# Two heads at a time in the indexer and the sparse logits, the keys' low half on 64 rows of the array each

## The chip, the cores and the metric

The kernel runs on one NeuronCore of a Trainium2 chip. The metric is the device time of one execution in microseconds (us). Before the change the median of three runs is 2247.49 us (2243.25 to 2249.33). The kernel and its change are compared on the same inputs, and only the time is in question.

## What is computed

The reference is one layer of a decoder trunk on 1024 positions of width 1024: a SwiGLU block, a projection into two attention mixers, the gated merge of both, and a second SwiGLU block. Two places matter here, both in the first mixer (sparse attention). For each block of 128 queries:

```python
dots = jnp.einsum('bthd,bsd->bths', qi, k_idx)               # 8 heads of 64, one key for all heads
score = jnp.einsum('bths,bth->bts', jax.nn.relu(dots), wi)   # the indexer's score of each key
...                                                          # causal mask, the 256 best keys stay
logits = jnp.einsum('bthd,btkd->bthk', qa, kg) * (HEAD_DIM ** -0.5)
p = jax.nn.softmax(logits, axis=-1)
```

The kernel does not gather the chosen keys. It makes the logits of all keys up to the block's own and adds a bias that hides those not chosen. In both places eight heads of 64 numbers are multiplied with the same keys.

## The kernel before

All matmuls read their float32 operands in the fast one-pass form, which keeps fewer digits, so an operand is stored as a high part and a low part, the rest, and a product of two such operands is three matmuls: high by high, low by high, high by low (`mm3`, L308 to L310). Heads have only 64 rows, half of the array's 128. So for each head the query tile holds its high part in 64 rows and its low part in the other 64; the keys' high part is stored twice, once in each half of the rows, and so is the low part. One matmul with the keys' high tile then gives two of the three products at once, and one with the keys' low tile gives the third, along with the product of the two low parts, which is too small to matter. In `qstack` (L1512, L1514) head h has its high part in the rows of half h % 2, and its low part in the other half.

The order of the work is made while the program is built. Generators ("streams") such as `indexer`, `logits` or `outputs` yield before each step and name the engine and what they need; the class `Weave` keeps an estimated clock of every engine (`cost`, L112) and always takes the step that can start first, by rank where two can. Each engine then runs its instructions in that order. Everything between the two SwiGLU blocks is ordered so, in these stretches (times from the trace):

- **Index**, about 788 to 903 us. `indexer` (L1546) goes through blocks of queries 5, 4, 2, 7, 6, 3, in each through 8 heads, and in each head through pieces of at most 512 keys. A piece is two matmuls into one bank of PSUM, `psdot` (L1560 with the keys' high part `kih`, L1561 with the low part `kil`). `dot_out` takes the bank: ACT writes its positive part (`relu`, L1530), DVE multiplies it by the head's weight and adds it to the score (L1535, L1537). Between these, `fillers` puts projection work on PE that nothing waits for at once (`psf`, `psvb`: L308 to L310).
- **Search and stick-breaking**, about 903 to 1262 us. `topk` finds the 256th score by 31 steps, each one ACT pass per block (L1183) and two small DVE steps. `sticks` and `values` do the second mixer. `fillers` goes on with the gates (`psf` with weights `wg`).
- **Sparse attention**, about 1262 to 1474 us. `logits` (L1809) makes the logits of blocks 1, 0, 5, 4, 7, 6, 3, 2, head by head, again two matmuls for each piece of 512 keys into a bank `psL` (L1828, L1829). `logit_out` (L1792, DVE) adds the bias and writes `e`; `soft` exponentiates on ACT and scales on DVE (L1807). `latent_values` turns `e` by transposes on PE (`pspT`, L1883) and multiplies with the values (`pso`). `outputs` gives PE work in between: the projection of the second mixer (`psob`), then of the first (`psoa`), which waits for the first's results.

The banks `psdot`, `psz` and `psL` come from one ring, `ubank`, of three PSUM banks. The tiles `e` come from three rings, two of four and two tiles and later a third of two.

Of the kernel before, what the change touches and what calls it, by code (L numbers as in the profile page):

```python
# [10 lines left out]
F32 = mybir.dt.float32  # L11
# [10 lines left out]
PE, DVE, ACT, POOL, SP = "PE", "DVE", "Activation", "Pool", "SP"  # L22

P = 128
# [6 lines left out]
H = 8  # L31
HD = 64
# [61 lines left out]
class Weave:  # L94
# [17 lines left out]
    def cost(self, i, eng, outs, ins):  # L112

        n = max([a.free_size() for a in outs[:1] + ins], default=1)
        if eng == PE:
            return 0.01 + max(outs[0].free_size(), 240) / 2350, 0.0
        if eng == ACT:
            return 0.055 + n / 1190 + 0.31 * (len(outs) > 1), 0.1 + 0.1 * (len(outs) > 1)
        if eng == POOL:
            return 0.2 + n / 465 + (0.15 + 0.145 * n) * (n <= H), 0.0  # L120
        wide = [a for a in outs[:1] + ins if a.free_size() > H]
        if not wide:
            return 0.12 + 0.1 * (len(ins) > 1), 0.08
        if getattr(i, "is_tensor_tensor_scan", False):
            return 0.1 + n / 480, 0.08
        if len(outs) > 1:
            return 0.13 + n / 960, 0.05
        if len(wide) == 2 and not any(a.space == PSUM for a in wide):
            return 0.17 + n * (0.5 if any(a.dtype in (F32, F32R, I32) for a in wide) else 0.25) / 960, 0.08
        slow = getattr(i, "is_scalar_tensor_tensor", False) or len(ins) == 1 and len(outs[0].shape) == 2 and n > outs[0].free_size()  # L130
        return 0.07 + 0.06 * slow + 0.11 * (outs[0].shape[0] < P) + n / 960, 0.08
# [51 lines left out]
    def mark(self, name, *needs):  # L183
        self.marks[name] = needs
# [23 lines left out]
    def spawn(self, gen, rank=1, own=None):  # L208
        s = Stream(gen, rank, own or self.own)
        self.streams.append(s)  # L210
        self.step(s)
        return s
# [33 lines left out]
def trunk(ctx, tc, x, positions, g_ffn1, w1_gate, w1_up, w1_down, g_mix, w_in, g_cq, w_uq_a, w_q_idx,  # L246
          g_q_a, g_k_a, w_uv_a, w_o_a, w_o_b, w_out, g_ffn2, w2_gate, w2_up, w2_down, inv_freq, out):
    nc = tc.nc
# [18 lines left out]
    def sm(name, n=1, dt=F32, bufs=4):  # L267
        return small.tile([P, n], dt, name=name, bufs=bufs)
# [479 lines left out]
    def ring(pool):  # L748

        op = in_turn((wt, 4), (lambda name: pool.tile([P, 1024], F32R, tag="r", name=name, bufs=NR), NR))  # L750
        raw = in_turn((rawt, 2), (lambda name: pool.tile([P, 1024], F32, tag="raw", name=name, bufs=2), 2))
        return op, raw
# [6 lines left out]
    with tc.tile_pool(name="ring1", bufs=1) as rpool, tc.tile_pool(name="s1", bufs=1) as spool, tc.tile_pool(name="ps1", bufs=1, space=PSUM) as psum:  # L759
        op, raw = ring(rpool)  # L760
        bank = banks(psum)
        sums, pair = of(spool, "s", 5, 512), of(spool, "pair", 2, 512, F32R)
# [197 lines left out]
    with fp as fpool, fps as fpsum, psm as psum, tc.manual_schedule(  # L960
            engines={nc.tensor.engine, nc.vector.engine, nc.scalar.engine, nc.gpsimd.engine}):
        weave = Weave(nc)
        give, spawn, mark = weave.give, weave.spawn, weave.mark
# [29 lines left out]
        ubank, vbank, wbank = (ring_of(tiles_of(psum), tag, bufs, (P, 512)) for tag, bufs in (("u", 3), ("v", 2), ("w", 1)))  # L993
# [7 lines left out]
        score, here, HQ, KV, QA, BIAS = {}, {}, [], [], [], []  # L1001
# [319 lines left out]
        KX, QI, WQ = {}, {}, {}  # L1321
# [196 lines left out]
        def index_queries():  # L1518
# [4 lines left out]
            give(*WQ["qi"].parts)  # L1523
            mark("wqi")

        def dot_out(ps, i, h, c0, w, acc, before):
            yield ACT, ps, relus
            rt = relus("relu")
            r = rt[:, 0:w]
            nc.scalar.activation(r, ps[:, 0:w], AF.Relu)  # L1530
            give(ps)
            yield DVE, rt, before
            wv, ac = WI[:, i, h:h + 1], acc[:, c0:c0 + w]
            if h == 0:
                nc.vector.tensor_scalar(ac, r, wv, None, op0=ALU.mult)  # L1535
            else:
                nc.vector.scalar_tensor_tensor(ac, r, wv, ac, op0=ALU.mult, op1=ALU.add)  # L1537
            give(rt)
# [7 lines left out]
        def indexer():  # L1546

            for i in order:
                yield PE, "kidx", f"qi{i}"
                nk = (i + 1) * P  # L1550
                acc = keep(f"u{i}", f"u{i}", 1, shape=(P, nk))
                outs = {}
                for h in range(H):
                    for c0 in range(0, nk, 512):
                        w = min(512, nk - c0)
                        yield PE, ubank
                        ps = ubank("psdot")
                        lh = QI[i][:, h * P:(h + 1) * P]
                        x = max(w, 256)
                        nc.tensor.matmul(ps[:, 0:x], lh, KX["h"][:, c0:c0 + x], start=True, stop=False)  # L1560
                        nc.tensor.matmul(ps[:, 0:x], lh, KX["l"][:, c0:c0 + x], start=False, stop=True)  # L1561
                        outs[c0] = spawn(dot_out(ps, i, h, c0, w, acc, outs.get(c0)))
                give(QI[i])
                score[i] = acc
                mark(f"score{i}", spawn(score_out(i, acc, list(outs.values()))))
# [41 lines left out]
        pring, lefts = ring_of(rows_, "pt", 3, dt=F32R), ring_of(rows_, "left", 2)  # L1607
        arings = ring_of(s, "a0", 4, (P, 512)), ring_of(rows_, "a1", 4)
# [180 lines left out]
        def logit_out(lp, e, bias, c0, n_, m):  # L1789
            yield DVE, lp  # L1790
            c = slice(c0, c0 + n_)
            nc.vector.tensor_tensor_reduce(e[:, c], lp[:, 0:n_], bias[:, c], 1.0, LOW, op0=ALU.add, op1=ALU.max,  # L1792
                                           accum_out=m)
            give(lp, bias)
# [14 lines left out]
        def logits():  # L1809
            n = 0  # L1810
            yield PE, "sparse", "ka2"
            kah, kal = KV[:2]
            for b, i in enumerate(blocks):
                nk = (i + 1) * P
                yield PE, f"qa{b}", f"bias{b}"
                QS, bias = QA[b], BIAS[b]
                for h in range(H):
                    rings = [arings[1], lefts] + ([here["e"]] if "e" in here else [])
                    yield PE, rings
                    ring = min(rings, key=lambda r: weave.when((r,), PE))  # L1820
                    e, mx, outs = ring("e"), sm("mx", 2, F32, 8), []
                    for g, c0 in enumerate(range(0, nk, 512)):
                        yield PE, ubank
                        lp = ubank("psL")
                        n_ = min(512, nk - c0)
                        w = max(n_, 256)
                        lh = QS[:, h * P:(h + 1) * P]
                        nc.tensor.matmul(lp[:, 0:w], lh, kah[:, c0:c0 + w], start=True, stop=False)  # L1828
                        nc.tensor.matmul(lp[:, 0:w], lh, kal[:, c0:c0 + w], start=False, stop=True)  # L1829
                        outs.append(spawn(logit_out(lp, e, bias, c0, n_, mx[:, g:g + 1])))  # L1830
                    E[n] = e
                    mark(f"p{n}", spawn(soft(n, e, nk, mx, outs)), e)
                    n += 1
                give(QS)

        def o_out(op, b, g):
# [333 lines left out]
```

## Time and profile before

| | |
|---|---|
| median of three runs | 2247.49 us |
| the profiled execution's own time | 2252.81 us |
| its span, first to last instruction | 2251.0 us |
| granted TensorE clock, mean | 0.987 |
| PE busy | 2175.0 us, 10460 matmuls |
| DVE busy | 1541.6 us |
| ACT busy | 1116.5 us |

The profile is of one execution. A matmul's duration in it reaches beyond the start of the next, since matmuls are pipelined: what a matmul costs in a stream is the distance from its start to the next one's start. PE stands for matmuls, PEld for the loads of their left-hand operand, which run beside them. In a row of the tiles' view the three numbers after the colon are the least, median and largest duration in ns. In a row of the windows' view the first number after the window is its length, then come the busy time and the number of instructions of PE, PEld, DVE, ACT and POOL, the granted clock, the share of the DMA engines' time, and GB/s. In a row of the timeline stand the start, the duration, the engine, the line, the operation with its result and operands, and how many of them were merged; idle time before it stands in brackets. In a row of the waits stand the total, the number of times, and the longest.

### The profile page before, as it was taken

Reading aid. Unit: us, or ns where it says so; the run is one execution under the profiler, and the core shown is the slowest. Engines: PE = TensorE matmul, PEld = TensorE weight load, DVE = VectorE, ACT = ScalarE, POOL = GpSimd, SP = SyncE. Lnnn points to the kernel's source line nnn. Section 1 sums busy time; section 2 is a strip of 40 time slices with the busy share of each in tenths; the row PEclk is TensorE's granted clock in tenths of the full one; section 3 lists DMA queues with packets and bytes.
Section 4 is the critical chain, followed back from the end, with each engine's and each line's share of the span. In section 5 each row is a group of like instructions: output and inputs, shape, how many; then the busy total and the mean of one; then the engine's idle time right before and its main releaser. Section 6 shows DMA issues by size and latency. Waiting matters only on the chain.

```text
span 2251.0 us, 30640 instructions
## 1 busy us (share of the span) xinstructions
PE 2175.0 (97%) x10460; PEld 1810.2 (80%) x10460; DVE 1541.6 (68%) x2548; ACT 1116.5 (50%) x2169; POOL 840.3 (37%) x698
## 2 busy tenths in 40 slices
PE   7999899999999999899999899999999999999999
PEld 6778777888878988788888788878878888888877
DVE  5866675677876498687787688853476565658685
ACT  5433333334445258999988466533333333334443
POOL 3554454522336344211111323255255555442233
PEclk9999999999999999999999999999999999999999
DMA  5377677678676333665555523566223332359655
GB/s 170 99 225 210 206 220 207 188 248 281 204 209 175 110 121 136 207 170 162 163 148 166 207 92 99 176 222 224 66 89 113 93 114 90 112 169 310 226 163 183
DMA packets 269052, 381.01 MB, mean 169 GB/s; under 512 B 23264, under 2 KB 157040, under 8 KB 268896
## 3 DMA queue, kind: packets, MB, share of 16 engines
q1 hardware_dynamic: 256384, 339.17, 49.0%
q0 software_dynamic: 12512, 39.89, 4.8%
q8 instruction: 82, 1.34, 0.3%
q14 instruction: 74, 0.61, 0.1%
HBM read 259.94 MB, written 119.05 MB: 168 GB/s over the span
## 4 chain that ended last, share of the span: by engine, by line
PE 63%; DVE 8%; ACT 7%; issue 3%; DMA 3%; POOL 1%; SPq 0%; ACTq 0%; DVEq 0%; POOLq 0%
PE p L678 5%; PE p L679 5%; PE p L677 5%; ACT junka L1183 4%; PE pc L467 2%; PE pc L468 2%; PE pc L469 2%; PE pd L467 2%; PE pd L469 2%; PE pd L468 2%; PE pa L467 2%; PE pa L469 2%; PE pa L468 2%; PE psf L308 2%; PE psf L309 2%
## 5 line engine op out<-in xcount | busy, mean ns | idle before, releaser
L1183 ACT ACTIVATE junka<-u,cand,sig 128x768 bf16<-128x768 f32 (+4 forms) x186 | 183.6, 987 | 5.6 <-DVE cand L1180 4.0
L1624 DVE TENSOR_TENSOR_SCAN left<-left 128x640 f32<-128x640 f32 (+3 forms) x64 | 86.3, 1348 | 4.0 <-ACT left L1616 4.0
L1117 POOL DMA_DIRECT2D gd<-evg x32 | 17.9, 558 | 152.7 <-ACT evg L1114 112.8
L1673 DVE TENSOR_TENSOR pt<-pstT,pt 128x512 fp32r<-128x512 f32 (+1 forms) x96 | 50.8, 549 | 28.6 <-ACT pt L1671 28.3
L786 ACT ACTIVATE swh<-swr 128x512 fp32r<-128x512 f32 x48 | 30.1, 626 | 71.3 <-PE pa L469 20.9
L1673 DVE TENSOR_TENSOR pt<-pspT,pt 128x512 fp32r<-128x512 f32 x72 | 46.8, 684 | 15.9 <-ACT pt L1671 15.9
L787 DVE TENSOR_TENSOR swr<-swr,swh 128x512 f32<-128x512 f32 x48 | 42.9, 893 | 19.2 <-ACT swh L786 19.1
L678 PE MATMUL p<-bT,bS 128*128 128x512 f32 x132 | 52.0, 394 | 2.8 <-DVE bT L378 2.8
L1792 DVE CUSTOM_DVE_ANT_0 e<-psL,bias 128x512 f32<-128x512 f32 (+3 forms) x96 | 49.7, 550 | 7.0 <-PE psL L1829 7.0
L1671 ACT ACTIVATE pt<-pspT 128x512 fp32r<-128x512 f32 x72 | 39.8, 596 | 29.6 <-PE pspT L1883 29.5
L1804 ACT ACTIVATE e<-e,nm 128x256 f32<-128x256 f32 (+7 forms) x64 | 49.3, 773 | 9.2 <-DVE nm L1799 8.7
L1537 DVE SCALAR_TENSOR_TENSOR u<-relu,WI,u 128x512 f32<-128x512 f32 (+1 forms) x70 | 50.0, 733 | 5.0 <-ACT relu L1530 4.4
L679 PE MATMUL p<-bT,bS 128*128 128x512 f32 x132 | 51.9, 395 | 1.0 <-POOL bS L378 1.0
L582 ACT ACTIVATE a0u<-a0u 128x512 f32<-128x512 f32 x20 | 12.6, 632 | 79.7 <-DVE a0u L490 45.0
L678 PE MATMUL p<-aT,aS 128*128 128x512 f32 x132 | 51.5, 390 | 0.1
L1627 DVE TENSOR_TENSOR sa<-sa,left 128x639 f32<-128x639 f32 (+3 forms) x64 | 48.1, 752 | 3.7 <-ACT sa L1618 0.3
L679 PE MATMUL p<-aT,aS 128*128 128x512 f32 x132 | 50.5, 390 | 0.0
L1530 ACT ACTIVATE relu<-psdot 128x512 f32<-128x512 f32 (+1 forms) x80 | 40.1, 519 | 17.2 <-DVE u L1537 8.5
L1671 ACT ACTIVATE pt<-pstT 128x512 fp32r<-128x512 f32 (+1 forms) x96 | 46.8, 515 | 3.2 <-PE pstT L1727 3.1
L1883 PE MATMUL pspT<-ident,e 128*128 128x128 f32 x288 | 40.1, 279 | 7.9 <-DVE ri L1806 5.5
L1618 ACT ACTIVATE sa<-psz 128x512 f32<-128x512 f32 (+2 forms) x96 | 46.9, 510 | 0.1
L1616 ACT ACTIVATE left<-psz 128x512 f32<-128x512 f32 (+2 forms) x96 | 46.1, 504 | 1.6 <-PE psz L1651 1.4
(3021 smaller groups left out, 8252.8 us busy)
## 6 DMA issues: line engine op xcount, KB each, us to landing
aw<-in_w_down_dram SPq DMA_DIRECT2D x33, 512.0 KB, 4.6
bw<-in_w_down_dram SPq DMA_DIRECT2D x33, 512.0 KB, 4.3
swr<-in_w_in_dram SPq DMA_DIRECT2D x48, 256.0 KB, 5.4
a0r<-in_w_gate_dram SPq DMA_DIRECT2D x22, 512.0 KB, 5.4
a1r<-in_w_up_dram SPq DMA_DIRECT2D x22, 512.0 KB, 6.2
b0r<-in_w_gate_dram SPq DMA_DIRECT2D x22, 512.0 KB, 4.1
b1r<-in_w_up_dram SPq DMA_DIRECT2D x22, 512.0 KB, 4.8
x<-in_x_dram SPq DMA_DIRECT2D x16, 512.0 KB, 6.4
```

What stands on the lines that cost most here:

```text
L467: nc.tensor.matmul(ps, a[:, c], b[k][:, HI], start=start and k == 0, stop=False, skip_group_check=True)
L468: nc.tensor.matmul(ps, a[:, c], b[k][:, LO], start=False, stop=False, skip_group_check=True)
L469: ins = nc.tensor.matmul(ps, a[:, l], b[k][:, HI], start=False, stop=k == 3, skip_group_check=True)
L677: nc.tensor.matmul(ps[q][m], S[:, h], T[:, HI], start=p == 0, stop=False)
L678: nc.tensor.matmul(ps[q][m], S[:, h], T[:, LO], start=False, stop=False)
L679: nc.tensor.matmul(ps[q][m], S[:, l], T[:, HI], start=False, stop=p == last)
L1183: nc.scalar.activation(junks[1][:, 0:(i + 1) * P], score[i], AF.Sign, scale=sig[:, b:b + 1], bias=cand.bitcast(F32)[:, b:b + 1], accum_out ...
L1537: nc.vector.scalar_tensor_tensor(ac, r, wv, ac, op0=ALU.mult, op1=ALU.add)
L1624: nc.vector.tensor_tensor_scan(back, back, back, 1.0, op0=ALU.mult, op1=ALU.bypass)
L1671: nc.scalar.activation(pt[:, off:512], tp[:, off:512], AF.Copy)
L1673: nc.vector.tensor_sub(pt[:, 512 + off:1024], tp[:, off:512], f32(pt[:, off:512]))
L1792: nc.vector.tensor_tensor_reduce(e[:, c], lp[:, 0:n_], bias[:, c], 1.0, LOW, op0=ALU.add, op1=ALU.max, accum_out=m)
```

## The change

Heads are taken two at a time, for each piece of keys. A new function makes four matmuls into two banks: both heads with the keys' high part, as before on all 128 rows; then both heads with the keys' low part, of which each uses only the 64 rows that hold its own high part. Head 0 of a pair has them in rows 0 to 63, head 1 in rows 64 to 127. The product of the two low parts is no longer made.

```diff
+        def two_heads(Q, kh, kl, h, c0, x, name):
+            pair = [(ubank(name), e) for e in range(2)]
+            lh = [Q[:, (h + e) * P:(h + e + 1) * P] for e in range(2)]
+            for ps, e in pair:
+                nc.tensor.matmul(ps[:, 0:x], lh[e], kh[:, c0:c0 + x], start=True, stop=False)
+            for ps, e in pair:
+                r = slice(e * HD, (e + 1) * HD)
+                nc.tensor.matmul(ps[:, 0:x], lh[e][r], kl[r, c0:c0 + x], start=False, stop=True)
+            return pair
...
 (indexer)
-                for h in range(H):
+                for h in range(0, H, 2):
                     for c0 in range(0, nk, 512):
                         w = min(512, nk - c0)
-                        yield PE, ubank
-                        ps = ubank("psdot")
-                        lh = QI[i][:, h * P:(h + 1) * P]
-                        x = max(w, 256)
-                        nc.tensor.matmul(ps[:, 0:x], lh, KX["h"][:, c0:c0 + x], start=True, stop=False)
-                        nc.tensor.matmul(ps[:, 0:x], lh, KX["l"][:, c0:c0 + x], start=False, stop=True)
-                        outs[c0] = spawn(dot_out(ps, i, h, c0, w, acc, outs.get(c0)))
+                        yield PE, (ubank, 2)
+                        for ps, e in two_heads(QI[i], KX["h"], KX["l"], h, c0, max(w, 256), "psdot"):
+                            outs[c0] = spawn(dot_out(ps, i, h + e, c0, w, acc, outs.get(c0)))
```

`logits` is changed in the same way: two tiles `e` are taken first, then for each piece of keys `(ubank, 2)` and `two_heads`, then both heads' `soft` are spawned. A pair needs two free banks of the three. The builder's estimate of a matmul on fewer than 128 rows is halved (`cost`); nothing else in `Weave` is changed, but since the estimates and the steps differ, the order of everything after the first pair does too. The numbers of matmuls (10460) and of the steps on ACT, DVE and POOL stay as they were.

On PE, in the indexer's first blocks, these instructions stand one after another before the change (`psdot` is the indexer, `psf` the filling projection, `pskt` transposes of the keys):

```order
L1560 MATMUL psdot<-kih,qsi 128x256
L1561 MATMUL psdot<-kil,qsi 128x256
L1560 MATMUL psdot<-kih,qsi 128x512
L1561 MATMUL psdot<-kil,qsi 128x512
L308 MATMUL psf<-mhi_5623,wqk5200h 128x512
L309 MATMUL psf<-mlo_5631,wqk5200h 128x512
L310 MATMUL psf<-mhi_5623,wqk5200l 128x512
L1447 MATMUL pskt<-ident,kdup 128x128 x4
L1560 MATMUL psdot<-kih,qsi 128x256
L1561 MATMUL psdot<-kil,qsi 128x256
```

and these in the same place with the change:

```order
L1531 MATMUL psdot<-kih,qsi 128x512 x2
L1534 MATMUL psdot<-kil,qsi 128x512 x2
L308 MATMUL psf<-mhi_5624,wqk5200h 128x512
L309 MATMUL psf<-mlo_5632,wqk5200h 128x512
L310 MATMUL psf<-mhi_5624,wqk5200l 128x512
L308 MATMUL psf<-mhi_5625,wqk5200h 128x512
L309 MATMUL psf<-mlo_5633,wqk5200h 128x512
L310 MATMUL psf<-mhi_5625,wqk5200l 128x512
L1447 MATMUL pskt<-ident,kdup 128x128 x4
L1531 MATMUL psdot<-kih,qsi 128x256 x2
L1534 MATMUL psdot<-kil,qsi 128x256 x2
```

The two matmuls of L1534 are those on 64 rows. In front of them always stand matmuls on all 128 rows, if only the pair's own with the keys' high part, and behind them too, so the array goes from 128 rows to 64 and back once for every pair. The indexer has 40 pairs and the logits 48: 88 pairs and 176 such changes in the whole program.

On PE, in the sparse attention, the last projection work `psob` ends so before the change (`pso` multiplies with the values, `pspT` are the transposes of `e`, `psya` the step behind `pso`):

```order
L1883 MATMUL pspT<-ident,e 128x128 x8
L1828 MATMUL psL<-kkh,qs 128x512
L1829 MATMUL psL<-kkl,qs 128x512
L308 MATMUL psob<-ybh_12177,ob6h 128x512
L309 MATMUL psob<-ybl_12181,ob6h 128x512
L310 MATMUL psob<-ybh_12177,ob6l 128x512
L1863 MATMUL pso<-pt,kkh 128x512
L1864 MATMUL pso<-pt,kkl 128x512
L1865 MATMUL pso<-pt,kkh 128x512
```

and with the change so:

```order
L310 MATMUL psob<-ybh_12167,ob6l 128x512
L1870 MATMUL pso<-pt,kkh 128x512
L1871 MATMUL pso<-pt,kkl 128x512
L1872 MATMUL pso<-pt,kkh 128x512
L1870 MATMUL pso<-pt,kkh 128x512
L1871 MATMUL pso<-pt,kkl 128x512
L1872 MATMUL pso<-pt,kkh 128x512
L1890 MATMUL pspT<-ident,e 128x128 x8
```

Before, 9 heads' logits still come after the last `psob`: one of block 3 and all of block 2. With the change it is 16 heads, all of blocks 3 and 2, in 8 pairs. So `psob` is used up earlier against the logits, and the last pairs stand among `pspT` and `pso` alone.

More of the change, by code (lines that the diff above doesn't have):

```diff
@@ L115, in cost @@
         if eng == PE:
-            return 0.01 + max(outs[0].free_size(), 240) / 2350, 0.0
+            return (0.01 + max(outs[0].free_size(), 240) / 2350) * (0.5 if min(a.shape[0] for a in ins) < P else 1), 0.0
         if eng == ACT:
@@ L1816, in logits @@
                 QS, bias = QA[b], BIAS[b]
[L1817 to L1821, printed above, removed]
+                for h in range(0, H, 2):
+                    es, mxs, outs = [], [], ([], [])
+                    for _ in range(2):
+                        rings = [arings[1], lefts] + ([here["e"]] if "e" in here else [])
+                        yield PE, rings
+                        ring = min(rings, key=lambda r: weave.when((r,), PE))
+                        es.append(ring("e"))
+                        mxs.append(sm("mx", 2, F32, 8))
                     for g, c0 in enumerate(range(0, nk, 512)):
-                        yield PE, ubank
-                        lp = ubank("psL")
+                        yield PE, (ubank, 2)
                         n_ = min(512, nk - c0)
[L1826 to L1833, printed above, removed]
+                        for lp, a in two_heads(QS, kah, kal, h, c0, max(n_, 256), "psL"):
+                            outs[a].append(spawn(logit_out(lp, es[a], bias, c0, n_, mxs[a][:, g:g + 1])))
+                    for a in range(2):
+                        E[n] = es[a]
+                        mark(f"p{n}", spawn(soft(n, es[a], nk, mxs[a], outs[a])), es[a])
+                        n += 1
                 give(QS)
```

## The prediction

> **What bounds the kernel now.** I read the page's first part, then the windows' view cut where the work changes, then the waits.
>
> ```profile
> PE 2175.0 (97%) x10460; PEld 1810.2 (80%) x10460; DVE 1541.6 (68%) x2548; ACT 1116.5 (50%) x2169; POOL 840.3 (37%) x698
> ```
> ```profile
> 788.00:903.00 115.00, 113.15 (x591) 96.26 (x590) 103.01 (x190) 81.77 (x171) 51.48 (x53) 0.98 0.38 128
> 903.00:943.00 40.00, 33.28 (x165) 27.37 (x164) 22.93 (x67) 37.26 (x72) 13.34 (x20) 0.87 0.59 185
> 943.00:1217.00 274.00, 271.87 (x1416) 220.67 (x1415) 218.47 (x413) 263.57 (x592) 37.33 (x68) 1.00 0.57 168
> 1217.00:1262.00 45.00, 44.91 (x221) 37.31 (x219) 27.39 (x81) 22.98 (x46) 8.37 (x12) 1.00 0.48 163
> 1262.00:1282.00 20.00, 12.15 (x49) 10.63 (x50) 13.84 (x60) 13.11 (x37) 4.91 (x6) 0.74 0.76 285
> 1282.00:1474.00 192.00, 187.91 (x1021) 158.38 (x1019) 155.60 (x433) 110.29 (x226) 54.31 (x48) 1.00 0.41 134
> ```
>
> PE is busy 97% of the span. Both stretches that the change touches are PE's: 113.15 of 115 us in the indexer (first row), 187.91 of 192 us in the sparse attention (last row). In the indexer DVE is close behind with 103.01. From 903 to 1217 us ACT is full as well (37.26 of 40, 263.57 of 274), while PE works off fillers; from 1217 to 1262 us PE has only them, and ACT 22.98 of 45. So a microsecond saved on PE in the indexer comes back if the fillers then end a microsecond sooner, at 1262; there the gap of 1262 to 1282 begins, whose length hangs on what follows the fillers' end.
>
> ```profile
> PE psdot L1560 <- ACT relu L1530: 1.9, 3, 1.2
> PE pspT L1883 <- DVE ri L1806: 5.5, 1, 5.5
> ```
>
> The waits say the same: the indexer's matmuls waited for a free bank three times, 1.9 us in all, and the logits' never. The 5.5 us are that gap's.
>
> **The change part by part.** First, what it removes. These are the matmuls with the keys' low half, and their distances in a stream:
>
> ```profile
> L1561 PEld LDWEIGHTS psdot<-kil,qsi x80: 187/188/338, 788.5 to 898.7; 128*128 128x128 f32 x80
> L1561 PE MATMUL psdot<-kil,qsi x80: 274/389/628, 789.0 to 899.0; 128*128 128x512 f32 x48, 128*128 128x256 f32 x16, 128*128 128x384 f32 x16
> L1829 PE MATMUL psL<-kkl,qs x96: 274/389/415, 1223.1 to 1440.2; 128*128 128x512 f32 x48, 128*128 128x256 f32 x32, 128*128 128x384 f32 x16
> ```
> ```profile
> 803.18 0.28 PE L1560 MATMUL psdot<-kih,qsi 128*128 128x256 f32 x1
> 803.29 0.28 PE L1561 MATMUL psdot<-kil,qsi 128*128 128x256 f32 x1
> 803.41 0.40 PE L1560 MATMUL psdot<-kih,qsi 128*128 128x512 f32 x1
> ...
> 825.39 0.33 PE L1560 MATMUL psdot<-kih,qsi 128*128 128x384 f32 x1
> 825.56 0.34 PE L1561 MATMUL psdot<-kil,qsi 128*128 128x384 f32 x1
> 825.74 0.33 PE L1560 MATMUL psdot<-kih,qsi 128*128 128x384 f32 x1
> ...
> 1250.19 0.39 PE L308 MATMUL psf<-mhi,wg6h 128*128 128x512 f32 x1
> ...
> 1261.52 0.39 PE L310 MATMUL psf<-mhi,wg7l 128*128 128x512 f32 x1
> ```
>
> Between the last two rows lie 50 steps of 512 columns: 11.33 / 50 = 0.227 us each. 256 columns take (803.41 - 803.18) / 2 = 0.115, 384 take (825.74 - 825.39) / 2 = 0.175. The indexer's low halves cost 48 x 0.227 + 16 x 0.115 + 16 x 0.175 = 15.5 us, the logits' 48 x 0.227 + 32 x 0.115 + 16 x 0.175 = 17.4 us. If the two of a pair run in the two halves of the array at the same time, half of that goes: 7.8 + 8.7 = **16.5 us**. If they run one after the other, nothing goes, since a matmul's time follows its columns in these rows and not its rows. No matmul of this trace uses fewer than 128 rows (every form begins with 128*128), so 0 and 16.5 are the bounds. I take 16.5: the two use different rows and different banks, and no row speaks against their running together.
>
> The Trainium skill bears on this (TensorE: Matmul & The Clock Gate, Part 3, the table of measured speedups): matmuls in different row groups run concurrently, and four of 32 rows gave 3.07 times. As an estimate from that page, four take 1.30 times one, so a partner costs a tenth, and the saving would be 14.8 us and not 16.5; no row here shows it.
>
> Second, what it adds. For each of the 88 pairs the array goes from 128 rows to 64 and back, 176 changes. The nearest rows are a change of another kind, a small bf16 matmul between two on fp32:
>
> ```profile
> 941.09 0.28 PE L1647 MATMUL psz<-kkh,qs 128*128 128x256 f32 x1
> 941.21 0.23 PE L1649 MATMUL psz<-tri 128*128 128x128 bf16 x1
> 941.25 0.36 PE L1651 MATMUL psz<-kkl,qs 128*128 128x256 f32 x1
> 941.45 0.39 PE L1647 MATMUL psz<-kkh,qs 128*128 128x512 f32 x1
> ```
> ```profile
> 810.31 0.60 PE L1503 MATMUL psqt<-ident,qx 128*128 128x128 f32 x4
> 810.67 0.48 PE L308 MATMUL psf<-mhi,wqk5200h 128*128 128x512 f32 x1
> ```
>
> From 941.09 to 941.45 are 0.36 us; two times 0.115 leave 0.13 for 128 columns of bf16 and two changes. Four transposes of 128 columns take 0.36, so 0.09 each; at that, 0.04 is left for two changes. At half of 0.115 it is 0.07. So a change there costs 0.02 to 0.035 us, and I take 0.025. The lower bound is nothing (a gain is excluded, since no row of the stream shows less than its columns). For the upper bound, a change could wait until the array is empty: the part of a matmul's 389 ns (rows of L1561 and L1829) that the next one now overlaps, 0.389 - 0.227 = 0.162 us. If the load of the left operand (188 ns, the row of PEld), which now lies under the matmul before, had to wait as well, it is 0.35. I take the bf16 rows, since they are the only ones in which the array is set up differently from one matmul to the next: 176 x 0.025 = **4.4 us**.
>
> Third, what moves. A pair waits for two of three banks. Before the next pair PE needs the earlier pair's first bank back, and the evictions take:
>
> ```profile
> L1530 ACT ACTIVATE relu<-psdot x80: 271/582/623, 789.6 to 902.7; 128x512 f32<-128x512 f32 x48, 128x384 f32<-128x384 f32 x16, 128x256 f32<-128x256 f32 x8, 128x128 f32<-128x128 f32 x8
> ```
> ```profile
> L1673 DVE TENSOR_TENSOR pt<-pspT,pt 128x512 fp32r<-128x512 f32 x19 | 12.2, 682 | 4.6 <-ACT pt L1671 4.6
> L1792 DVE CUSTOM_DVE_ANT_0 e<-psL,bias 128x512 f32<-128x512 f32 x9 | 5.8, 682 | 0.0
> ```
>
> In the indexer the next pair comes after three to six fillers (the order quoted above), 0.7 to 1.4 us, which hides one 0.58 us pass; I cost it at nothing. Without fillers it would be some 0.6 us a pair, 24 us for 40 pairs. In the logits `psob` covers it, until it is used up. Behind that stand eight pairs with `pspT` and `pso` alone, and DVE has little left there:
>
> ```profile
> 1420.00:1440.00 20.00, 19.73 (x117) 17.12 (x116) 19.00 (x59) 13.97 (x34) 4.23 (x3) 1.00 0.68 239
> ```
>
> DVE's work does not shrink (0.68 us for each bank of `psL` and of `pspT`), so what these eight pairs save, 4 x 0.227 + 4 x 0.175 = 1.6 us, I count as lost, and 0.9 more for the pairs' waits: **2.5 us**, between 0 and 5.5 (as much as the longest of the waits above).
>
> The search's ACT passes are the other thing to look at, because blocks 5, 4 and 2 must be scored before they begin:
>
> ```profile
> L1183 ACT ACTIVATE junka<-u,cand,sig x186: 694/998/1297, 849.5 to 1235.6; 128x768 bf16<-128x768 f32 x31, 128x640 bf16<-128x640 f32 x31, 128x384 bf16<-128x384 f32 x31, 128x1024 bf16<-128x1024 f32 x31
> ```
>
> They end at 1235.6, 26 us ahead of the fillers' end. Fillers that end 7 us sooner still end later than they do. If they began 19 us later, this cover would be gone and each further microsecond would count. DMAs, POOL's and SP's steps are the same in number.
>
> The sum: 16.5 - 4.4 - 2.5 = 9.6 us less. Against the profiled execution (2252.81 us, of which the span is 2251.0) that is 2243.2; its median is 5.3 lower, and from 2247.5 it gives **2238**. About 0.3% (6.7 us) is what a measurement of this kernel can tell from no change.
>
> **The rivals.** *Slower: the array is emptied at each change of rows.* The place is the 176 changes, the price 0.162 us each, 28.5 us; with the 16.5 and the 2.5 that is 14.5 us more, 2262. It decides from (16.5 - 2.5) / 176 = 0.08 us a change on. For it: a matmul now runs 0.162 us beyond the start of the next, and no row shows that this overlap holds where the next one uses other rows of the array. Against it: the bf16 rows, and the transposes, after which the projection goes on with no gap. With the loads exposed too it would be 61.6 us and 2295. The Trainium skill states this rival as a rule (TensorEngine Tiling (Array Packing), Key Properties): "Mode switching requires drain: Changing tiling mode (not just tile) drains the TensorE". It names no time, and no run here shows it yet. Chance 0.28, of which 0.07 for the loads exposed.
>
> *The halves do not run together.* Then 0 - 4.4, and about 1 us for the waits: 5.4 us more, 2253. For it: no row shows two matmuls at once. Chance 0.10.
>
> *The indexer's part is not paid out.* DVE has 103.01 of its 115 us filled and ACT 263.57 of 274 behind it; if they hold back the scores, the 7.8 us become idle time of PE: 16.5 - 7.8 - 4.4 - 2.5 = 1.8 us less, 2246. Against it: the fillers, which PE takes instead, up to 1262. Chance 0.12.
>
> **How the numbers follow.** The forecast has 0.50: 2238, its own range 2231 (nothing for the changes, nothing for the waits) to 2245 (twice the taken price, 0.05, for a change, and 5.5 for the waits: 16.5 - 8.8 - 5.5 = 2.2 less). About three quarters of it, 0.38, lie under 2240.8 and are faster; 0.12 are the same. Of the second rival 0.06 are the same and 0.04 slower, of the third all 0.12 the same, of the first 0.26 slower and 0.02 the same. That makes 0.38 faster, 0.32 the same, 0.30 slower. The range goes from 2231, under which the whole saving would have to come with no cost, to 2263, which takes in the emptied array; above it are the exposed loads and part of the case before, some 0.12.
>
> **What would show it.** In the profile after: the two matmuls of L1534 start within some 0.05 us of each other, and the next matmul starts some 0.25 us after the first of them and not 0.45 (concurrent, at 512 columns); the distance from a pair's last full matmul to its first half one is 0.25 and not 0.39 (no emptying). The fillers' last `psf` should end near 1256, the step from 1282 to 1474 should shrink by 3 to 6 us, and 903 to 1217 should stay PE- and ACT-full. The prediction is wrong if a change costs over 0.08 us, if the two run one after the other, or if idle time of PE before `psdot`, `psL` or `pspT` grows by over 5 us.

## The result and the profile after

| | before | after |
|---|---|---|
| median | 2248.41 us, 4 runs (2243.25 to 2252.05) | 2278.23 us, 4 runs (2277.69 to 2279.95) |
| the profiled execution's own time | 2252.81 us | 2278.23 us |
| its span | 2251.0 us | 2276.5 us |

The change costs 29.8 us between the medians; the ratio after to before on record is 1.0138, with a 95% interval of 1.0125 to 1.0151 (the medians alone give 1.0133). The kernel before has one run more here than in the prediction, so its median is 2248.41 and not 2247.49. The forecast was 2238, and the range ended at 2263.

The page's first part after the change, in the same columns as before:

```profile
PE 2196.1 (96%) x10460; PEld 1793.6 (79%) x10460; DVE 1543.1 (68%) x2548; ACT 1118.8 (49%) x2169; POOL 841.7 (37%) x698
```

The work of DVE, ACT and POOL is unchanged to within 2.3 us. PE is busy 21 us longer, although 88 of its steps were to go. So I look at PE first, at one pair among fillers (timeline, matmuls and then loads):

```profile
801.79 0.39 PE L309 MATMUL psf<-mlo,wqk5200h 128*128 128x512 f32 x1
802.02 0.40 PE L310 MATMUL psf<-mhi,wqk5200l 128*128 128x512 f32 x1
802.25 0.62 PE L1531 MATMUL psdot<-kih,qsi 128*128 128x512 f32 x2
802.80 0.50 PE L1534 MATMUL psdot<-kil,qsi 64*128 64x512 f32 x2
803.23 0.50 PE L308 MATMUL psf<-mhi,wqk5200h 128*128 128x512 f32 x1
803.57 0.39 PE L309 MATMUL psf<-mlo,wqk5200h 128*128 128x512 f32 x1
803.80 0.40 PE L310 MATMUL psf<-mhi,wqk5200l 128*128 128x512 f32 x1
...
802.02 0.42 PEld L1531 LDWEIGHTS psdot<-kih,qsi 128*128 128x128 f32 x2
802.80 0.19 PEld L1534 LDWEIGHTS psdot<-kil,qsi 64*128 64x128 f32 x2 [0.36 <-issue]
803.23 0.19 PEld L308 LDWEIGHTS psf<-mhi,wqk5200h 128*128 128x128 f32 x1 [0.25 <-issue]
803.34 0.19 PEld L309 LDWEIGHTS psf<-mlo,wqk5200h 128*128 128x128 f32 x1
803.58 0.19 PEld L310 LDWEIGHTS psf<-mhi,wqk5200l 128*128 128x128 f32 x1
```

Three things are to be seen.

- **The halves run together.** Both matmuls of L1534 stand in one row of 0.50 us, which is what each of them takes alone (the median of 498 ns below). Their two starts lie 3 ns apart at the median of all 88 pairs. From the first of them to the next full matmul it still takes 0.43 us, so the proof that the second costs no time of its own is the experiment below in which the low halves are made twice.
- **At each change of rows the next matmul waits for the last one.** The pair's second full matmul starts at 802.25 + 0.62 - 0.39 = 802.48, and the half ones 0.32 us after it, where 0.227 were enough for 512 columns: 0.09 more. They begin when the last full one is all but over (802.48 + 0.39 = 802.87). This fits an array that is emptied first; since the ends are modelled, the trace does not show the emptying itself.
- **The load is exposed.** Elsewhere a left operand is loaded under the matmul before: L310's begins at 803.58, its matmul at 803.80. At a change the load starts together with its own matmul, at 802.80 and again at 803.23, after 0.36 and 0.25 us of nothing on PEld, and the matmul takes 0.50 instead of 0.39: 0.11 more. That second row is the change back to 128 rows, which costs the same.

The whole price of one pair: from 802.25 to 803.57 are 1.32 us for four steps of 512 columns (two full ones, the pair at once, one filler), which need 4 x 0.227 = 0.91. So a pair costs **0.41 us** beyond its columns, 0.205 for each change, and saves one step, 0.227. With 512 columns it loses 0.18 us, with 384 0.41 - 0.175 = 0.23, with 256 0.41 - 0.115 = 0.29. The indexer and the logits have 48 pairs, 16 and 24 of these: 48 x 0.18 + 16 x 0.23 + 24 x 0.29 = 19 us lost. The tiles' view has it for all pairs:

```profile
L1534 PE MATMUL psdot<-kil,qsi x80: 379/498/792, 785.7 to 910.8; 64*128 64x512 f32 x48, 64*128 64x256 f32 x16, 64*128 64x384 f32 x16
...
L1534 PE MATMUL psL<-kkl,qs x96: 379/492/792, 1237.1 to 1467.2; 64*128 64x512 f32 x48, 64*128 64x256 f32 x32, 64*128 64x384 f32 x16
```

The median was 389 ns in both places before; now even the shortest, of 256 columns, takes 379, where it was 274.

In the windows' view, cut where the work changes now:

```profile
788.00:910.00 122.00, 120.97 (x616) 90.50 (x615) 102.46 (x188) 80.68 (x167) 49.79 (x53) 0.99 0.32 112
910.00:943.00 33.00, 26.56 (x120) 21.24 (x119) 19.39 (x57) 28.77 (x57) 9.87 (x13) 0.90 0.48 165
943.00:1217.00 274.00, 271.69 (x1403) 219.51 (x1402) 213.93 (x406) 263.69 (x585) 38.32 (x71) 1.00 0.58 172
1217.00:1265.00 48.00, 48.00 (x242) 39.52 (x241) 32.92 (x91) 31.42 (x65) 9.50 (x14) 1.00 0.48 152
1265.00:1305.00 40.00, 29.36 (x97) 19.76 (x97) 29.34 (x112) 20.27 (x54) 5.46 (x7) 0.66 0.49 181
1305.00:1500.00 195.00, 188.32 (x974) 144.71 (x973) 146.60 (x388) 105.23 (x211) 54.01 (x47) 0.99 0.38 126
```

PE stays full in the indexer (120.97 of 122) and in the logits: the changes of rows show as busy time, not as idle time. But not all of the loss is there. From 1265 to 1305, behind the fillers' end, PE does 97 matmuls at a granted clock of 0.66. Before the change, the 40 us behind its fillers' end were:

```profile
1261.50:1301.50 40.00, 31.62 (x149) 26.47 (x148) 30.26 (x119) 25.27 (x64) 14.82 (x15) 0.87 0.63 222
```

149 matmuls there, 97 now. As an estimate from these two rows, 40 us at a clock of 0.66 hold 8.4 us less of full clock than at 0.87. So a second cause, the order, is suspected beside the first. In the waits, `ri` and `e` before `pspT` (5.5 us before, in the prediction, and 2.4 us, the first row) have grown by 2.9 us together:

```profile
PE pspT L1883 <- DVE e L1807: 2.4, 2, 1.9
PE pspT L1890 <- DVE ri L1813: 6.0, 1, 6.0
PE pspT L1890 <- DVE e L1814: 4.8, 4, 1.9
```

### The profile page after: what moved, and what is told of

Same layout as the page of the kernel before. It is cut to its first block, busy times and chain, and to the rows that moved or that the text cites. A ratio compares the mean times of both kernels' runs of the same rounds, so it can differ in the third digit from the quotient of the medians.

```text
span 2276.5 us, 30665 instructions
## 1 busy us (share of the span) xinstructions
PE 2196.1 (96%) x10460; PEld 1793.6 (79%) x10460; DVE 1543.1 (68%) x2548; ACT 1118.8 (49%) x2169; POOL 841.7 (37%) x698
## 4 chain that ended last, share of the span: by engine, by line
PE 68%; ACT 5%; DVE 5%; DMA 3%; issue 3%; POOL 1%; SPq 0%; ACTq 0%; DVEq 0%; POOLq 0%
PE p L678 5%; PE p L679 5%; PE p L677 5%; PE psf L308 3%; ACT junka L1183 3%; PE psf L309 3%; PE psf L310 3%; PE pc L467 2%; PE pc L468 2%; PE pc L469 2%; PE pd L467 2%; PE pd L468 2%; PE pd L469 2%; PE pa L468 2%; PE pa L469 2%
## 5 line engine op out<-in xcount | busy, mean ns | idle before, releaser
L1183 ACT ACTIVATE junka<-u,cand,sig 128x1024 bf16<-128x1024 f32 (+5 forms) x186 | 184.2, 990 | 9.4 <-DVE cand L1180 6.4
L1680 DVE TENSOR_TENSOR pt<-pstT,pt 128x512 fp32r<-128x512 f32 (+1 forms) x96 | 51.0, 549 | 23.3 <-ACT pt L1678 23.0
L786 ACT ACTIVATE swh<-swr 128x512 fp32r<-128x512 f32 x48 | 30.1, 626 | 73.1 <-PE pa L469 25.2
L1548 DVE SCALAR_TENSOR_TENSOR u<-relu,WI,u 128x512 f32<-128x512 f32 (+3 forms) x70 | 51.0, 736 | 9.0 <-ACT relu L1541 7.2
L1541 ACT ACTIVATE relu<-psdot 128x512 f32<-128x512 f32 (+3 forms) x80 | 40.3, 520 | 27.4 <-PE psdot L1534 16.3
L1890 PEld LDWEIGHTS pspT<-ident,e 128*128 128x128 f32 x288 | 35.5, 146 | 18.8 <-issue 7.5
```

The lines of the kernel that those rows point to most:

```text
L1183: nc.scalar.activation(junks[1][:, 0:(i + 1) * P], score[i], AF.Sign, scale=sig[:, b:b + 1], bias=cand.bitcast(F32)[:, b:b + 1], accum_out ...
L1680: nc.vector.tensor_sub(pt[:, 512 + off:1024], tp[:, off:512], f32(pt[:, off:512]))
L1890: nc.tensor.transpose(tp[:, q * P:(q + 1) * P], E[n + q][:, j * P:(j + 1) * P], ident)
```

## The experiments

Each kernel is compared with the kernel before on the same chip in the same batch (medians of 2247.35 to 2247.75 us), and "+x us" is the difference from that. The first theory (A) is that the changes of rows are the cause; its rival (B), that the new order is. Where something stayed with full rows as well, A1 puts it down to the halved estimate, and A2 to taking two heads at a time.

### The order kept, the rows full

The program after, instruction for instruction in the same order, but each low half on all 128 rows; the builder's estimate is halved by name, so that the order stays.

```diff
-                r = slice(e * HD, (e + 1) * HD)
-                nc.tensor.matmul(ps[:, 0:x], lh[e][r], kl[r, c0:c0 + x], start=False, stop=True)
+                nc.tensor.matmul(ps[:, 0:x], lh[e], kl[:, c0:c0 + x], start=False, stop=True)
```

> The changed kernel's order, instruction by instruction, but the low-half matmuls use all 128 rows again, so the array never changes its rows. Theory A (the changes of rows cost the time: about 0.41 us a pair beyond the columns, 88 pairs, 36 us, less 16.5 us saved by running together): 2252 to 2260 us, that is 19 us or more under the changed kernel's 2278. Rival B (taking two heads at a time makes an order that leaves PE waiting, whatever the rows): 2270 to 2280 us.

Measured: 2262.51 us (2257.36 to 2264.74), ratio 1.0064 [1.0049, 1.0079], +14.8 us. That is between the two. Without any change of rows half of the loss is still there; the 64 rows themselves cost 29.8 - 14.8 = 15.0 us. Neither theory alone holds. The traces have the same 10460 matmuls in the same order in both kernels.

### The rows halved, the order kept from before

The kernel before, heads one by one, but each low half on the 64 rows of its head: 176 excursions to 64 rows, and no partner to run beside.

```diff
-                        nc.tensor.matmul(ps[:, 0:x], lh, KX["l"][:, c0:c0 + x], start=False, stop=True)
+                        r = slice(h % 2 * HD, (h % 2 + 1) * HD)
+                        nc.tensor.matmul(ps[:, 0:x], lh[r], KX["l"][r, c0:c0 + x], start=False, stop=True)
```

> The kernel before with its own order, one head at a time, but each low-half matmul on the 64 rows that hold the head's high part: 176 changes to 64 rows and 176 back, no two running together. Theory A: 176 x 0.41 = 72 us more than before, about 2320 us. Rival B: the order is that of before, so the time is that of before within a few us, about 2250.

Measured: 2320.81 us (2315.11 to 2324.71), ratio 1.0324 [1.0306, 1.0343], +73.1 us. Worked out: 176 x 0.41 = 72.2. Nothing moved here and nothing can run side by side, so the price of an excursion is shown by itself. Its timeline:

```profile
804.10 0.51 PE L1560 MATMUL psdot<-kih,qsi 128*128 128x512 f32 x1
804.53 0.49 PE L1562 MATMUL psdot<-kil,qsi 64*128 64x512 f32 x1
804.95 0.50 PE L308 MATMUL psf<-mhi,wqk5200h 128*128 128x512 f32 x1
805.29 0.39 PE L309 MATMUL psf<-mlo,wqk5200h 128*128 128x512 f32 x1
```

Each matmul behind a change shows 0.49 to 0.51 us. Where another change follows it, the next one starts 0.42 to 0.43 us after it; behind the last change that is 0.34, where 0.227 are the columns.

### The low halves twice

The program after, in its order, but each pair's two low halves are made twice, one pair right behind the other, so that the low product counts twice in the result. If 64 rows are slow as such, or if each load stays exposed, the second pair costs what the first does; if the price is in the change, only its columns. The builder's clock passes over the added matmuls, so that the order stays; the lines that do this are left out below.

```diff
+            for n in range(2):
                 for ps, e in pair:
                     r = slice(e * HD, (e + 1) * HD)
-                    nc.tensor.matmul(ps[:, 0:x], lh[e][r], kl[r, c0:c0 + x], start=False, stop=True)
+                    nc.tensor.matmul(ps[:, 0:x], lh[e][r], kl[r, c0:c0 + x], start=False, stop=n == 1)
...
```

> The changed kernel's order with each pair's low halves made twice, right after each other, into the same banks (so the product with the low half counts twice in scores and logits): 176 more 64-row matmuls, but no more changes of rows. If the price lies in the change of rows, the second pair costs its columns alone, half of 33 us: 2278 + 16.5 = 2295 us. Rival (each 64-row pair costs the 0.41 us, whether the rows change or not): 2278 + 16.5 + 36 = 2330 us, or 2314 if the 0.41 hold the columns.

Measured: 2291.89 us (2291.48 to 2292.91), ratio 1.0195 [1.0179, 1.0211], +44.5 us, 14.7 more than after, where the columns alone ask for 16.5. The price is in the change. In its timeline the four half matmuls stand in one row, and so do their loads:

```profile
809.06 0.71 PE L1534 MATMUL psdot<-kih,qsi 128*128 128x512 f32 x2
809.70 0.73 PE L1538 MATMUL psdot<-kil,qsi 64*128 64x512 f32 x4
810.36 0.50 PE L311 MATMUL psf<-mhi,wqk5200h 128*128 128x512 f32 x1
...
809.70 0.30 PEld L1538 LDWEIGHTS psdot<-kil,qsi 64*128 64x128 f32 x4 [0.36 <-issue]
```

From 809.70 to the next full matmul it takes 0.66 us, where one pair took 0.43: the second pair adds 0.23, one step of 512 columns for two matmuls: this shows that the two of a pair cost the time of one. All four loads are done at 810.00, so the second pair's lie under the first pair's matmuls.

### One place alone

Only the indexer in pairs, `logits` as before the change; and only the logits in pairs, `indexer` as before it.

```diff
 (logits, in the first)
-                for h in range(0, H, 2):
+                for h in range(H):
...
 (indexer, in the second)
-                for h in range(0, H, 2):
+                for h in range(H):
...
```

> The change in the indexer alone, the logits as before. Theory A: 40 pairs x 0.41 = 16.4 less 7.8 saved = 8.6 us more than before, about 2257 us. Rival B, if the order at the start of the sparse attention is the cause: 2248 to 2252.

> The change in the sparse logits alone, the indexer as before. Theory A: 48 pairs x 0.41 = 19.7 less 8.7 saved = 11 us, and the longer stretch at half clock where the logits begin, some 10 us: 2265 to 2272 us. Rival B: the same or more, up to 2278; the two parts tell apart where the time goes, not which of the two it is.

Measured: the indexer alone 2264.25 us (2259.53 to 2267.89), ratio 1.0075 [1.0057, 1.0094], +16.5; the logits alone 2272.23 (2267.91 to 2275.03), ratio 1.0109 [1.0093, 1.0124], +24.5. Each loses by itself. The indexer alone costs 8 us more than theory A's 8.6, and more than the rival allowed as well; the logits alone come to the upper end of A's range. Their sum, 41.0, is 11 us more than both together cost, so not all of what each costs is counted per pair. That would fit an order that is simply another one each time; these two runs do not show it.

### The estimate told the truth

The program after with 0.2 us added to the builder's estimate of each 64-row matmul; and the order that this gives, with full rows.

```diff
-            return (0.01 + max(outs[0].free_size(), 240) / 2350) * (0.5 if min(a.shape[0] for a in ins) < P else 1), 0.0
+            t = 0.01 + max(outs[0].free_size(), 240) / 2350
+            return (t / 2 + 0.2 if min(a.shape[0] for a in ins) < P else t), 0.0
```

> The changed kernel with 64 rows and pairs as they are, but the builder's estimate of a low-half matmul is no longer halved: half its columns' time plus 0.2 us, about what the trace shows. The scores then stand earlier against the fillers, and psob before the first transposes of e. Theory A1 (of the 30 us some 19 are the changes of rows and the rest comes from the order that the halved estimate made: the scores, and with them the search, end later against the fillers): 2264 to 2270 us. Rival A2 (the rest comes from taking heads in pairs, whatever the estimate): 2276 to 2280 us.

> The same order as the kernel with the corrected estimate, instruction by instruction, with the low halves on all 128 rows. Theory A1: 2246 to 2252 us, as before the change, and 15 to 20 us under the kernel with the corrected estimate on 64 rows. Rival A2: 2260 to 2264, as with pairs on full rows in the changed kernel's order.

Measured: 2270.69 us (2267.88 to 2272.29), ratio 1.0099 [1.0081, 1.0116], +23.3; with full rows 2258.30 (2256.84 to 2260.47), ratio 1.0046 [1.0028, 1.0063], +11.0. The truth wins back 6.5 us of 29.8, and between these two equal orders the 64 rows cost 12.4 us. But the second was to come near the kernel before, by A1 (2246 to 2252), and did not, nor is it in A2's range. Behind its fillers' end it is better than before (35.08 us of PE busy in 40, against 31.62):

```profile
1267.20:1307.20 40.00, 35.08 (x156) 26.75 (x155) 23.77 (x91) 22.80 (x58) 18.41 (x17) 0.87 0.74 254
```

It loses in other places instead, around the indexer's start for one, where 4.3 us of these waits before (first row) have become 9.6, and before `psob`, which now waits 4.8 us for its operands' DMA and did not before. These places were not tried one by one.

```profile
PE psqt L1503 <- DVE qx L1499: 4.3, 2, 3.1
PE psqt L1504 <- DVE qx L1500: 9.6, 3, 4.6
PE psob L310 <- DMA ybl<-ybld: 3.6, 4, 1.5
PE psob L309 <- DMA ybh<-ybhd: 1.2, 2, 0.7
```

### Pairs on full rows with the estimate from before

The program after with each low half on all 128 rows, as in the first experiment, and `cost` as it was before the change:

```diff
-            return (0.01 + max(outs[0].free_size(), 240) / 2350) * (0.5 if min(a.shape[0] for a in ins) < P else 1), 0.0
+            return 0.01 + max(outs[0].free_size(), 240) / 2350, 0.0
```

> Pairs of heads on all 128 rows, and the builder's estimate as it was before the change. Theory A1: the first psob still stands behind 24 transposes of e and the scores end somewhat later than before the change, so between the kernel before and the one with pairs in the changed kernel's order: 2250 to 2260 us. Rival A2: 2260 to 2264 us.

Measured: 2256.08 us (2251.58 to 2259.29, 8 runs), ratio 1.0038 [1.0025, 1.0050], +8.7 us. The halved estimate accounts for 14.8 - 8.7 = 6.1 us. Two heads at a time leave 8.7, with every matmul as it was.

### What of a pair costs

Two ways to take a pair apart, both with full rows and the estimate from before. In the first the four matmuls go head by head (high, low, high, low), both banks still taken at once; in the second each head's piece waits for one bank, so that fillers may come between.

```diff
 (the first)
-            lh = [Q[:, (h + e) * P:(h + e + 1) * P] for e in range(2)]
             for ps, e in pair:
-                nc.tensor.matmul(ps[:, 0:x], lh[e], kh[:, c0:c0 + x], start=True, stop=False)
-            for ps, e in pair:
-                nc.tensor.matmul(ps[:, 0:x], lh[e], kl[:, c0:c0 + x], start=False, stop=True)
+                lh = Q[:, (h + e) * P:(h + e + 1) * P]
+                nc.tensor.matmul(ps[:, 0:x], lh, kh[:, c0:c0 + x], start=True, stop=False)
+                nc.tensor.matmul(ps[:, 0:x], lh, kl[:, c0:c0 + x], start=False, stop=True)
...
 (the second, in the logits; the same in the indexer)
-                        yield PE, (ubank, 2)
+                        for a in range(2):
+                            yield PE, ubank
...
```

> Heads in pairs, low halves on all 128 rows, the builder's estimate as before the change; within a pair the order on PE is head 0 high, head 0 low, head 1 high, head 1 low, where it was high, high, low, low (that version took 2256.1, 8.7 us over the kernel before). Both banks are still taken at once. If the order of the four matmuls costs something (the first bank is finished later in a high, high, low, low pair): 2248 to 2251. If the two banks taken at once, or the two heads, cost it: 2254 to 2260.

> Heads in pairs, 128 rows, estimate as before the change, but each head's piece is a step of its own that waits for one bank, so that filling work can come between the two heads. If the two banks at once are what pairing costs: 2246 to 2251. If it is the two heads (two tiles e taken early, two heads' scores side by side) or the order of everything behind them: 2253 to 2260.

Measured: 2257.74 us (2255.02 to 2259.19), ratio 1.0053 [1.0038, 1.0068], +10.0; and 2252.82 (2248.23 to 2255.68, 7 runs), ratio 1.0027 [1.0016, 1.0039], +5.1. The order within a pair shows no cost: 10.0 against 8.7 is within the noise of both. The second lies between its two cases: bank by bank is perhaps some us better than both at once, and yet slower than before by 3.6 to 8.8 us (0.0016 and 0.0039 of 2247.8).

### Another order without pairs

Two controls with single heads, in which no matmul and no step differs from the kernel before, only the estimate from which the order is made: the low halves' halved in the first, and all matmuls into `psdot` and `psL` raised by 5% in the second.

```diff
 (the first: low halves)
-            return 0.01 + max(outs[0].free_size(), 240) / 2350, 0.0
+            return (0.01 + max(outs[0].free_size(), 240) / 2350) * (0.5 if outs[0].tensor.name.startswith(("psdot", "psL")) and any(a.tensor.name.startswith(("kil", "kkl")) for a in ins) else 1), 0.0
...
 (the second: all of psdot and psL)
-            return 0.01 + max(outs[0].free_size(), 240) / 2350, 0.0
+            return (0.01 + max(outs[0].free_size(), 240) / 2350) * (1.05 if outs[0].tensor.name.startswith(("psdot", "psL")) else 1), 0.0
```

> The kernel before with one thing changed: the builder's estimate of the low-half matmuls is halved, as the change makes it; heads single, every matmul as before, only the order of the steps differs. If pairing alone costs: 2246 to 2250. If a wrong estimate costs by itself about what it added to pairs (2262.5 against 2256.1, some 6 us): 2252 to 2256. If any other order than the one before costs as much as pairing did: 2255 to 2262.

> A control: the kernel before with the estimate of all matmuls into psdot and psL raised by 5%, which makes another order out of the same steps for no reason at all. If pairing alone costs: 2246 to 2250. If the order of before is simply a favourable one and others cost: 2253 to 2262, as the versions with pairs on full rows did.

Measured: 2260.00 us (2258.21 to 2261.94), ratio 1.0067 [1.0050, 1.0084], +12.3; and 2254.06 (2250.88 to 2257.12), ratio 1.0031 [1.0014, 1.0049], +6.3. This takes the ground from A2: an order that is different for no reason costs 6.3 us with single heads, as much as pairs do with the plain estimate (5.1 to 10.0), and a halved estimate costs with single heads (12.3) about what it costs with pairs (14.8). What was left with full rows is put down to the order, then, from two such controls; a share of a few us for the pairs themselves can't be excluded, since the control's interval reaches from 3.1 to 11.0 us (0.0014 and 0.0049 of 2247.8).

Where the halved estimate tells is again behind the fillers' end. First the control with the halved estimate:

```profile
1254.20:1294.20 40.00, 23.30 (x91) 16.92 (x90) 34.68 (x127) 23.00 (x60) 5.46 (x7) 0.77 0.45 165
```
```profile
L308 PE MATMUL psob<-ybh,ob0h x16: 389/396/628, 1293.2 to 1317.3; 128*128 128x512 f32 x16
```

and then the other one, whose profiled execution took 2250.88 us, less than the profiled one before (2252.81), so that its views cannot show where its 6.3 us lie:

```profile
1261.60:1301.60 40.00, 30.48 (x160) 25.39 (x159) 36.06 (x120) 26.73 (x67) 16.34 (x16) 0.91 0.63 221
```
```profile
L308 PE MATMUL psob<-ybh,ob0h x16: 389/389/476, 1279.0 to 1296.3; 128*128 128x512 f32 x16
```

The first `psob` before the change, after it, and with pairs on full rows and the plain estimate:

```profile
L308 PE MATMUL psob<-ybh,ob0h x16: 389/389/396, 1280.9 to 1298.2; 128*128 128x512 f32 x16
```
```profile
L308 PE MATMUL psob<-ybh,ob0h x16: 389/476/793, 1299.1 to 1327.3; 128*128 128x512 f32 x16
```
```profile
L308 PE MATMUL psob<-ybh,ob0h x16: 389/397/632, 1287.0 to 1313.4; 128*128 128x512 f32 x16
```

With the halved estimate the fillers are used up at 1254.2 and the first `psob`, the next work that could fill PE, starts 39 us later, as after the change it starts 33.6 us behind the fillers' end (1265.5 to 1299.1); in the other control it is 17.4 us, and before the change 19.4 (1261.5 to 1280.9). After the change the operands of the first `psob` had landed by 1276.9 at the latest (the last of their transfers was issued at 1265.2 and none took over 11.7 us), and PE was not idle just before 1299.1: so it is its place in PE's order that makes it late. But this distance does not account for the losses of the other orders. Pairs on full rows with the plain estimate have 30.9 us (1256.1 to 1287.0) and lose 8.7; the true estimate's order on full rows has 0.3 (1267.2 to 1267.5) and loses 11.0. What makes one order slower than another stays open.

## Why the prediction was wrong

- **"If the two of a pair run in the two halves of the array at the same time, half of that goes": right.** They start 3 ns apart, and a second pair behind the first costs 0.23 us, one step of columns for two matmuls. The Trainium skill (TensorE: Matmul & The Clock Gate, Part 3, Measured speedup vs the span model) counts about 4 ns for the issue of each further tile; the trace agrees. The rival that the halves don't run together falls. The prediction's own sign for it, that the next matmul starts "some 0.25 us after the first of them and not 0.45", came out at 0.43 and would have told the opposite: it left out the 0.20 us that the changes of rows add between these two starts.
- **"I take the bf16 rows ...: 176 x 0.025 = 4.4 us": wrong, and the step that failed first.** A change of rows costs 0.205 us, 36.1 us for 176 of them. The row chosen shows a change of data type on all 128 rows, and what is slow is a change of rows. Both parts of the upper bound came true in a smaller size: the emptying 0.09 us (the next matmul begins before the modelled end of the last) where 0.162 was the bound, the load 0.11 where 0.188 was. The 0.205 is measured; how it divides into the two is a reading of the starts, and no run separates them. The price lies far above the 0.08 us that the text named as the point of decision, and the rival that it gave a chance of 0.28 is what happened, between its two prices of 2262 and 2295. The single heads on 64 rows show it by themselves: +73.1 us. "Mode switching requires drain", the Trainium skill's rule (TensorEngine Tiling (Array Packing), Key Properties), agrees with the trace as far as it goes: 0.09 us at each change in which the next matmul waits for the last, and 0.11 of load that the rule does not speak of.
- **"Third, what moves ... 2.5 us": wrong by more than three times.** With full rows the change costs 8.7 us by the old estimate, and 14.8 by the halved one, which gives the order that it has. I priced the moved work at the one place that the order showed, the eight last pairs. But the whole order behind the first pair is new, and in seven trials another order cost 5 to 15 us with every matmul on full rows (6.3 and 12.3 in the controls without pairs, 5.1 to 14.8 with pairs). The halved estimate, which made the builder believe in 16.5 us of saving that PE does not get, adds about 6 us to that (6.1 with full rows; 6.5 by telling it the truth).
- **"I cost it at nothing" (a pair's wait for two banks): right.** Before `psdot` PE waited 1.0 us in all after the change, 1.9 before. The row is from the tiles' view:

```profile
  ACT relu L1541: 1.0, 1
```

- **"They end at 1235.6, 26 us ahead of the fillers' end": a cover that was read too short a way.** The last pass now starts at 1250.2, 15 us ahead of 1265.5, so the cover of the passes held. Behind the last pass come DVE's steps that make the bias, whose last one starts at 1276.3 before and 1294.2 after, 15 and 29 us behind the fillers' end (first start to last start in the rows, before and after):

```profile
L1241 DVE TENSOR_SCALAR cum<-eq,rem x6: 304/386/486, 1174.7 to 1276.3; 128x768 bf16<-128x768 f16 x1, 128x640 bf16<-128x640 f16 x1, 128x384 bf16<-128x384 f16 x1, 128x1024 bf16<-128x1024 f16 x1
L1241 DVE TENSOR_SCALAR cum<-eq,rem x6: 320/392/486, 1192.4 to 1294.2; 128x768 bf16<-128x768 f16 x1, 128x640 bf16<-128x640 f16 x1, 128x384 bf16<-128x384 f16 x1, 128x1024 bf16<-128x1024 f16 x1
```

  How much of the loss behind the fillers' end is due to these steps was not tried. They are not all of what an order costs: on full rows with the true estimate the last one starts at 1266.0, ahead of the fillers' end at 1267.2, and 11.0 us are lost all the same.
- **The sum.** By full rows with the plain estimate, the halved estimate, and the 64 rows: 8.7 + 6.1 + 15.0 = 29.8 us. The three are differences between neighbouring runs, so they add up to the loss by construction, and each is uncertain by a few us. The 15.0 are 4 us less than the 19 worked out from the timeline, and 12.4 in the order with the true estimate: part of the time on PE may lie beside waits that are there anyway, which was not taken apart. With the right price for a change and its own 2.5 for the rest, the prediction's sum would have given 2247.5 - 16.5 + 36.1 + 2.5, about 2270; what is missing from there to 2278 is the order's 14.8 us, of which it had only 2.5, less the 4 us by which the changes of rows cost less than their price.
- Of the signs named, the fillers' end "near 1256" came at 1265.5, and the stretch from 1282 on grew. The idle time before `psL` and `pspT` grew by less than the 5 us named (2.9 before `pspT`); the price over 0.08 us alone would have told that the prediction was wrong.

No version that was run is faster than the kernel before.

## What to carry to other kernels

Two matmuls on half the rows do run at the same time, but going to half the rows and back costs as much as nearly two steps of 512 columns. As an estimate from 0.41 us for each excursion and the steps of 0.227, 0.175 and 0.115, a saving begins only where two pairs of 512 columns, three of 384 or four of 256 stand one right behind the other (as a gain this was not tried). A change between 128 and 64 rows is priced by a row with that very change, or else by its upper bound. Where a program's order is made from estimates, another order is a cost of its own: run a control with another order and no change, before the rest of a difference is put down to the change.

## What the runs showed of the hardware

- The price of a pair is the same for 256, 384 and 512 columns. At the median of all pairs the start of the half ones comes 212, 268 and 326 ns behind the last full one, 0.09 to 0.10 us beyond the columns; the next full one 318, 372 and 432 ns behind the half ones, 0.20 beyond the columns; and the matmul after that 0.11 later than the columns ask.
- A second pair on the same rows costs only its columns (0.23 us at 512), and its loads are hidden again.
- Single 64-row matmuls save nothing: each excursion costs 0.41 us, with one matmul in it or with two side by side.
